# The attention sink as a column of the score rows, and one softmax step for both halves of a block

## The chip, the cores and the metric

The kernel runs on one core of a Trainium2 chip. A core has a matmul engine (TensorE, here PE), three elementwise engines (VectorE or DVE, ScalarE or ACT, GpSimd or POOL), a sequencer that issues most of the transfers (SyncE, SP), and on-chip memories SBUF and PSUM; matmuls write PSUM. Each engine works through its own list of instructions in order and waits on semaphores for the others. The metric is the device time of one execution in microseconds, the median of the runs shown.

## The reference

One layer of a hybrid decoder, for 1024 prompt tokens and 64 sample tokens, width 1024. One input projection feeds a sliding-window attention group and a state-space (SSD) group; their outputs go through one output projection, then a gated FFN. The attention is what the change touches:

```python
def sink_attention(q, k, v, valid, sinks):
    s = jnp.einsum('bnqkgd,bnskd->bnkgqs', q, k) * (HEAD_DIM ** -0.5)
    s = jnp.where(valid[None, :, None, None], s, -jnp.inf)
    sink = sinks.reshape(1, 1, ATT_KV_HEADS, ATT_GROUP, 1, 1)
    m = jnp.maximum(jnp.max(s, axis=-1, keepdims=True), sink)
    p = jnp.exp(s - m)
    den = jnp.sum(p, axis=-1, keepdims=True) + jnp.exp(sink - m)
    return jnp.einsum('bnkgqs,bnskd->bnqkgd', p / den, v)
```

The sink is one learned score per head. It takes part in the maximum and in the denominator, and has no value vector. A prompt query sees its own block of 128 keys and the block before, so a row of scores is 256 wide (128 in the first block); a sample query sees 192.

## The kernel before

Full precision comes from split operands: each matrix is a high part and a low part, and `gemm` (L140 to L142) makes three matmul passes. The prompt is cut into chunks of 384, 384 and 320 columns (the last holds the sample tokens).

The stage of the change begins about 466 us into the span and ends about 775 us in. There `weave` runs two programs on PE: the mixer (`attention`, later `att_sample`) and the filler (the z projection of the SSD gate, and after it the first output projection). The mixer yields a number, the time for which the filler may hold PE before the mixer goes on. This sets PE's list of instructions by hand. The lists of DVE, ACT, POOL and SP are ordered by a scheduler, from the program order and priorities; `tc.high_priority()` marks the steps that PE waits for soonest.

Attention has 16 blocks (n, p): n = 0 to 7 is a block of 128 queries, p one of two groups of 8 heads. Tiles are named after p: `a_0...` and `a_1...`. Each block does:

- `blk_a` loads q, k, v (SP), transposes v on PE (L737, `a_pvt`), and splits k into `KW` (ACT L742, DVE L743) and q into `A` (ACT L749, POOL L750).
- `blk_b` makes the scores (PE L768, tile `a_ps`, two PSUM buffers of two heads each), in two halves e = 0, 1 of four heads. DVE L774 adds the mask to a head's scores, writes them into the SBUF tile `a_pS` (one per half, four buffers) and takes the row maximum into `a_pmx`; each is two instructions, the reduce and a read of its accumulator. Then comes `softmax` (L709 to L723) for this half: `nm` = -max(mx/8, sink) (L711, 128x4), `es` = nm + sink (L713) and its exponential (ACT L714), four exponentials with the row sum into `den` (ACT L718), den + es (L719), reciprocal (L720), and four scalings of the rows in place (DVE L723).
- `blk_c` of the block *before* follows the scores on PE: for each half of the keys eight transposes (L792, `a_pt`: four heads of half 0, then four of half 1), copied out of PSUM as `a_pPT` (L113: half 0 by DVE, half 1 by ACT), then the product with v (L800, `a_po`) and its copy to `of` (ACT L805).

So the scalings of one block have to be there when PE, after the next block's scores, comes to their transposes. In between, the group norm of the SSD output (`gate`, L926 to L963) runs in pieces on DVE, ACT and POOL: `gz`, `gy` are its tiles, `g0...` its small norm tiles of the first chunk (L174 to L184, 128x6, and the diagonals `g0d` of L203, 128x128), `g1...` of the second. The filler's results leave PSUM by DVE (`stg`, L486), its weights `wi_0`, `wi_1` (later `wos`, `woa`) are split by ACT (L123) and by POOL or DVE (L124). All of these stand in the same lists as the softmax.

Of the kernel before, what the change touches and what calls it, by code (L numbers as in the profile page):

```python
# [34 lines left out]
def hybrid_layer(ctx, tc, A):  # L35
# [26 lines left out]
    # split operands of a chunk in half tiles of four feature tiles each, in numbered slots  # L62
# [37 lines left out]
    class Extra:  # L100
        # weight slots cut out of a larger tile
# [31 lines left out]
    def gemm(out, ws, xs, step=3, only=None):  # L133
        # three passes of split operands; yields the time on the tensor engine
# [18 lines left out]
    def weave(mixer, filler):  # L153
        # the filler yields its time on the tensor engine, or None while its operands are not there;
        # the mixer yields how long the filler may hold the tensor engine before it goes on
        credit = 0.0
        for gap in mixer:
            credit += gap
            while credit > 0:
                try:  # L160
                    cost = next(filler)
                except StopIteration:
                    break
                if cost is None:
                    break
                credit -= cost
# [4 lines left out]
    def rsqrt_cols(st, nb, inv, name):  # L171
        # 1/sqrt(st * inv + eps), one token per partition: bit-level first guess, Newton to float32
# [14 lines left out]
    def rms(groups, n, inv, name, gap, keep=None):  # L187
        # groups of tiles; the sum over a group's tiles and partitions is the sum of squares of each token
# [40 lines left out]
    # scratch in DRAM  # L229
# [106 lines left out]
    with pool("conv") as cvp:  # L336
# [38 lines left out]
        with pool("norm") as tp:  # L375
# [15 lines left out]
            # the tensor engine's clock comes up while the first operands are on their way  # L391
# [11 lines left out]
            def dt_mm(c, k):  # L403
                # four feature tiles at a time, in four column groups of the array
# [19 lines left out]
            # the first chunk by feature tile, as they come in; its evacuation waits for the row scale  # L424
# [82 lines left out]
    with pool("ssd") as sd, pool("rope") as rp:  # L507
# [5 lines left out]
        def ssd_a(c, gi):  # L513
            # token-major x scaled by dt and by the tail decay; masked C.B; decay weights
# [194 lines left out]
    def softmax(ap, mx, name, nh, nsk, sk, tile_w):  # L709
        nm = ap.tile([P, nh], F32, tag="nm", bufs=2, name=name + "nm")  # L710
        v.scalar_tensor_tensor(nm, mx, -0.125, nsk, ALU.mult, ALU.min)  # L711
        es = ap.tile([P, nh], F32, tag="es", bufs=2, name=name + "es")
        v.tensor_add(es, nm, sk)  # L713
        s.activation(es, es, AF.Exp)  # L714
        den = ap.tile([P, nh], F32, tag="den", bufs=2, name=name + "den")
        for h in range(nh):
            w = tile_w(h)
            s.activation(w, w, AF.Exp, bias=nm[:, h:h + 1], scale=0.125, accum_out=den[:, h:h + 1])  # L718
        v.tensor_add(den, den, es)  # L719
        v.reciprocal(den, den)  # L720
        for h in range(nh):
            w = tile_w(h)
# [31 lines left out]
    def blk_b(ap, n, p, KW, Aqs):  # L754
# [3 lines left out]
        Sms = [ap.tile([P, 4, 2 * P], F32, tag="Sm", bufs=4, name=nm + "S%d" % e) for e in range(2)]  # L758
# [3 lines left out]
        for e in range(2):  # L762
            for g2 in range(2):
# [6 lines left out]
                for a in range(2):  # L770
                    gi = 2 * g2 + a
                    h = 4 * e + gi
                    with tc.high_priority():
                        v.tensor_tensor_reduce(Sms[e][:, gi, :W], sq_[:, a, :W], cst[:, mcol:mcol + W],  # L774
                                               1.0, -3.0e38, ALU.add, ALU.max, mx[:, h:h + 1])
                yield 0.6
            o = 4 * e
            softmax(ap, mx[:, o:o + 4], nm, 4, nsink[:, 8 * p + o:8 * p + o + 4],
                    vec[:, V_SINK + 8 * p + o:V_SINK + 8 * p + o + 4], lambda h: Sms[e][:, h, :W])
        return Sms  # L780

    def blk_c(ap, n, p, vts, Sms):
# [4 lines left out]
        for kt in range(nk):  # L787
            PTs = []
            for e in range(2):
                tp_ = ps("t", nm + "t")  # L790
                for gi in range(4):
                    t.transpose(tp_[:, gi * P:gi * P + P], Sms[e][:, gi, kt * P:kt * P + P], ident)  # L792
# [15 lines left out]
    nsink = sp.tile([P, 17], F32, name="nsink")  # L808
    v.tensor_scalar_mul(nsink, vec[:, V_SINK:V_SINK + 17], -1.0)
# [26 lines left out]
    # sampled tokens: one batch row at a time, all heads on the rows  # L836
    def att_sample(ap):
        Qb = [ap.tile([P, NB, P], F32, name="Qb%d" % p) for p in range(2)]
        cv = ap.tile([P, NB, 2 * P], F32, name="cv")
        Ss = ap.tile([P, NB, 192], F32, name="Ss")  # L840
# [32 lines left out]
        for b2 in range(4):  # L873
# [7 lines left out]
            for i in range(2):  # L881
                b = 2 * b2 + i
                with tc.high_priority():
                    v.tensor_tensor_reduce(Ss[:, b, :], scs[:, i, :], mk[:, b, :], 1.0, -3.0e38, ALU.add, ALU.max, mx[:, b:b + 1])
            yield 1.7
            if b2 % 2:
                o = 4 * (b2 // 2)
                softmax(ap, mx[:, o:o + 4], "as%d" % b2, 4, nsink[:, 16:17].broadcast_to([P, 4]),
                        vec[:, V_SINKS:V_SINKS + 1].broadcast_to([P, 4]), lambda h: Ss[:, o + h, :])
# [3 lines left out]
        def tr(b2):  # L893
            tp_ = ps("t", "as%dt" % b2)
            for i in range(2):
                t.transpose(tp_[:, 2 * P * i:2 * P * i + P], Ss[:, 2 * b2 + i, :P], ident)
                t.transpose(tp_[:NS, 2 * P * i + P:2 * P * i + 2 * P], Ss[:, 2 * b2 + i, P:], ident)
# [30 lines left out]
    def gate(c, at=None):  # L928
        # y * silu(z), its norm, and the split of the result
# [131 lines left out]
    with pool("chain") as kp:  # L1061
        # the first FFN tiles go chunk by chunk
# [23 lines left out]
    with pool("ffn") as fp:  # L1086
        # the cache rows that only move up, in the time when little else is loaded
# [5 lines left out]
        for gi, G in enumerate(FFG):  # L1093
# [51 lines left out]
            else:  # L1145
                # the last feature tiles go chunk by chunk, with the last norm and the residual behind them
# [163 lines left out]
```

## Time and profile before

| | |
|---|---|
| runs | 1766.32, 1768.01, 1768.69 us |
| median | 1768.01 us |
| span of the profiled execution | 1755.4 us |
| median less the span | 12.6 us |
| PE busy | 1650.0 us, 94% |
| DVE / ACT / POOL busy | 931.4 / 629.0 / 659.3 us (53 / 36 / 38%) |

The profiled execution has no time of its own beside the three runs; its span, from the first instruction to the last, is 12.6 us under the median, and this difference is carried along unchanged. An engine's busy time is what its instructions took; PE's share of 94% is a mean over stages. The trace names, for every instruction that had to wait, what came last of the things that it waited for; "idle before" is that waiting time.

### The profile page before, as it was taken

To read this page: it belongs to the slowest core of one execution; us is meant where nothing else is said; L and a number is where in the kernel's file an instruction comes from. 1 tells how busy PE (TensorE), PEld (TensorE's weight loads), DVE (VectorE), ACT (ScalarE), POOL (GpSimd) and SP (SyncE) were. 2 spreads that over 40 slices of the span, in tenths; PEclk is the share of its full clock that TensorE was granted. 3 is DMA by queue.
4 is the path that set the end of the run, shared out by engine and by line. 5 is a ranking of instruction groups with operands and counts; after the bars stand their busy time and mean duration, and the time that the engine had idled before them with its cause. 6 is when DMAs were issued, how large, how long until landed. Compare 5 with 4: busy or idle time off the path is not lost. (4 is left out here: it accounts for less than half of the span.)

```text
span 1755.4 us, 26644 instructions
## 1 busy us (share of the span) xinstructions
PE 1650.0 (94%) x9959; PEld 1553.4 (88%) x9959; DVE 931.4 (53%) x1977; ACT 629.0 (36%) x1416; POOL 659.3 (38%) x537
## 2 busy tenths in 40 slices
PE   9899998888888998999988999999999999999995
PEld 6899987766776787898987999999999999999995
DVE  7796778886588898455877401221312212121347
ACT  5242344441376676554543332112121121211221
POOL 5262366666743333323655322222222221221432
PEclk9899999998999999999999999999999999999997
DMA  5022564444652351543554111111111111110233
GB/s 184 30 85 101 166 177 136 134 125 157 208 153 84 93 156 59 167 148 94 180 179 141 47 49 32 49 52 32 55 41 47 44 38 49 41 55 22 82 102 102
DMA packets 144945, 171.12 MB, mean 97 GB/s; under 512 B 16624, under 2 KB 105200, under 8 KB 144784
## 3 DMA queue, kind: packets, MB, share of 16 engines
q1 hardware_dynamic: 144816, 169.43, 31.6%
q8 instruction: 78, 1.28, 0.3%
q14 instruction: 51, 0.42, 0.1%
HBM read 135.33 MB, written 36.28 MB: 98 GB/s over the span
## 5 line engine op out<-in xcount | busy, mean ns | idle before, releaser
L1027 DVE TENSOR_TENSOR sg<-sg,ou 128x384 f32<-128x384 f32 (+1 forms) x66 | 35.0, 531 | 393.4 <-PE ou L142 392.7
L1138 DVE TENSOR_TENSOR YP<-YP,od 128x384 f32<-128x384 f32 (+1 forms) x168 | 89.0, 531 | 126.9 <-PE od L142 126.7
L124 POOL TENSOR_TENSOR wg_1l<-wg_1r,wg_1h 128x512 fp32r<-128x512 f32 x20 | 25.9, 1295 | 211.5 <-ACT wg_1h L123 211.5
L1028 ACT CAST ffh<-sg 128x384 fp32r<-128x384 f32 (+1 forms) x66 | 32.6, 495 | 188.9 <-DVE sg L1027 188.5
L124 POOL TENSOR_TENSOR wi_1l<-wi_1r,wi_1h 128x512 fp32r<-128x512 f32 x40 | 56.7, 1418 | 63.7 <-ACT wi_1h L123 60.2
L1023 ACT ACTIVATE sg<-og 128x384 f32<-128x384 f32 (+1 forms) x66 | 31.0, 471 | 131.9 <-PE og L142 125.2
L124 POOL TENSOR_TENSOR wi_0l<-wi_0r,wi_0h 128x512 fp32r<-128x512 f32 x40 | 58.3, 1458 | 30.6 <-ACT wi_0h L123 26.2
L1029 DVE TENSOR_TENSOR ffl<-sg,ffh 128x384 fp32r<-128x384 f32 (+1 forms) x66 | 42.8, 649 | 33.9 <-ACT ffh L1028 33.8
L140 PE MATMUL ip<-x1h,wi_0h 128*128 128x384 f32 x128 | 48.0, 375 | 11.8 <-ACT ra L681 5.2
L124 POOL TENSOR_TENSOR wos_1l<-wos_1r,wos_1h 128x512 fp32r<-128x512 f32 x24 | 33.1, 1377 | 65.3 <-ACT wos_1h L123 58.3
L124 POOL TENSOR_TENSOR woa_1l<-woa_1r,woa_1h 128x512 fp32r<-128x512 f32 x24 | 35.0, 1456 | 49.6 <-ACT woa_1h L123 38.4
L363 DVE SCALAR_TENSOR_TENSOR cacc<-cbuf,vec,cacc 128x1112 f32<-128x1112 f32 x36 | 52.3, 1455 | 0.7
L140 PE MATMUL ip<-x0h,wi_0h 128*128 128x384 f32 x128 | 47.4, 371 | 3.5 <-DVE cbuf L350 3.5
L124 POOL TENSOR_TENSOR wd_1l<-wd_1r,wd_1h 128x384 fp32r<-128x384 f32 (+1 forms) x7 | 6.8, 974 | 105.2 <-ACT wd_1h L123 105.2
L140 PE MATMUL ip<-x0h,wi_1h 128*128 128x384 f32 x128 | 45.6, 356 | 0.0
L142 PE MATMUL ip<-x0h,wi_0l 128*128 128x384 f32 x128 | 44.0, 344 | 1.5 <-POOL wi_0l L124 1.5
L140 PE MATMUL ip<-x1h,wi_1h 128*128 128x384 f32 x128 | 45.1, 353 | 0.0
L124 POOL TENSOR_TENSOR wg_0l<-wg_0r,wg_0h 128x512 fp32r<-128x512 f32 x21 | 27.4, 1304 | 45.6 <-ACT wg_0h L123 45.6
L142 PE MATMUL ip<-x1h,wi_0l 128*128 128x384 f32 x128 | 44.3, 346 | 0.0
L141 PE MATMUL ip<-x0l,wi_0h 128*128 128x384 f32 x128 | 43.8, 342 | 0.4 <-DVE x0l L261 0.4
L141 PE MATMUL ip<-x1l,wi_0h 128*128 128x384 f32 x128 | 44.2, 345 | 0.0
L684 POOL TENSOR_TENSOR rb<-rb,sinT 128x384 f32<-128x384 f32 (+1 forms) x30 | 36.0, 1198 | 21.2 <-DVE rb L683 17.5
(837 smaller groups left out, 6215.0 us busy)
## 6 DMA issues: line engine op xcount, KB each, us to landing
wi_0r<-in_w_in SPq DMA_DIRECT2D x40, 256.0 KB
wi_1r<-in_w_in SPq DMA_DIRECT2D x40, 256.0 KB
wos_0r<-in_w_os SPq DMA_DIRECT2D x24, 256.0 KB
wos_1r<-in_w_os SPq DMA_DIRECT2D x24, 256.0 KB
woa_0r<-in_w_oa SPq DMA_DIRECT2D x24, 256.0 KB
woa_1r<-in_w_oa SPq DMA_DIRECT2D x24, 256.0 KB
wg_0r<-in_w_g SPq DMA_DIRECT2D x22, 256.0 KB
wg_1r<-in_w_g SPq DMA_DIRECT2D x22, 256.0 KB
```

The source lines that it names most:

```text
L124: (eng or g).tensor_sub(lo, raw, fr(hi))
L140: t.matmul(out, lhsT=wh, rhs=xh, start=k == 0, stop=False)
L141: t.matmul(out, lhsT=wh, rhs=xl, start=False, stop=False)
L142: t.matmul(out, lhsT=wl, rhs=xh, start=False, stop=k == n - 1)
L363: v.scalar_tensor_tensor(acc[:, :L], buf[:, k:k + L], vec[:, cw + k:cw + k + 1], acc[:, :L], ALU.mult, ALU.add)
L684: g.tensor_mul(b, b, sinT[:, c0:c0 + n])
L1023: s.activation(sg, og[:, :n], AF.Silu)
L1027: v.tensor_mul(sg, sg, ou[:, :n])
L1028: s.copy(hi[:, c0:c0 + n], sg)
L1029: v.tensor_sub(lo[:, c0:c0 + n], sg, fr(hi[:, c0:c0 + n]))
L1138: v.tensor_add(YP[m][:, c0:c0 + n], YP[m][:, c0:c0 + n], o[:, :n])
```

## The change

- A tile `sink8` holds eight times the sink of each head (scores are scaled by 1/8 in the exponential). The tile `nsink` is gone.
- `a_pS` grows from 4x256 to 4x257 columns for each half. Column 0 of each row is the sink, copied there by two POOL instructions of 128x4 per block (L757 of the new file); scores start at column 1. For the samples, `Ss` grows from 192 to 193 columns, and one DVE copy fills the column.
- The reduce (L773) starts its maximum from the sink, read per partition from `sink8`, in place of a constant.
- `softmax` is called once per block, after both halves: one `nm` (L712, 128x8), eight exponentials of 257 columns (L715), one reciprocal (L716, 128x8), eight scalings (L719) of the 256 columns behind the sink. `es`, its exponential and the addition to `den` are gone, since the row sum contains the sink.
- The transposes (L789) read from column 1 on.

```diff
-    def softmax(ap, mx, name, nh, nsk, sk, tile_w):
+    def softmax(ap, mx, name, nh, row):
         nm = ap.tile([P, nh], F32, tag="nm", bufs=2, name=name + "nm")
-        v.scalar_tensor_tensor(nm, mx, -0.125, nsk, ALU.mult, ALU.min)
-        es = ap.tile([P, nh], F32, tag="es", bufs=2, name=name + "es")
-        v.tensor_add(es, nm, sk)
-        s.activation(es, es, AF.Exp)
+        v.tensor_scalar_mul(nm, mx, -0.125)
         den = ap.tile([P, nh], F32, tag="den", bufs=2, name=name + "den")
         for h in range(nh):
-            w = tile_w(h)
-            s.activation(w, w, AF.Exp, bias=nm[:, h:h + 1], scale=0.125, accum_out=den[:, h:h + 1])
-        v.tensor_add(den, den, es)
+            s.activation(row(h), row(h), AF.Exp, bias=nm[:, h:h + 1], scale=0.125, accum_out=den[:, h:h + 1])
         v.reciprocal(den, den)
         for h in range(nh):
-            w = tile_w(h)
+            w = row(h)[:, 1:]
             v.tensor_scalar_mul(w, w, den[:, h:h + 1])
...
-        Sms = [ap.tile([P, 4, 2 * P], F32, tag="Sm", bufs=4, name=nm + "S%d" % e) for e in range(2)]
+        Sms = [ap.tile([P, 4, 2 * P + 1], F32, tag="Sm", bufs=4, name=nm + "S%d" % e) for e in range(2)]
+        for e in range(2):
+            o = 8 * p + 4 * e
+            g.tensor_copy(Sms[e][:, :, 0:1], sink8[:, o:o + 4].unsqueeze(2))
...
-                        v.tensor_tensor_reduce(Sms[e][:, gi, :W], sq_[:, a, :W], cst[:, mcol:mcol + W],
-                                               1.0, -3.0e38, ALU.add, ALU.max, mx[:, h:h + 1])
+                        v.tensor_tensor_reduce(Sms[e][:, gi, 1:1 + W], sq_[:, a, :W], cst[:, mcol:mcol + W],
+                                               1.0, sink8[:, 8 * p + h:8 * p + h + 1], ALU.add, ALU.max, mx[:, h:h + 1])
                 yield 0.6
-            o = 4 * e
-            softmax(ap, mx[:, o:o + 4], nm, 4, nsink[:, 8 * p + o:8 * p + o + 4],
-                    vec[:, V_SINK + 8 * p + o:V_SINK + 8 * p + o + 4], lambda h: Sms[e][:, h, :W])
+        softmax(ap, mx, nm, 8, lambda h: Sms[h // 4][:, h % 4, :1 + W])
         return Sms
...
-                    t.transpose(tp_[:, gi * P:gi * P + P], Sms[e][:, gi, kt * P:kt * P + P], ident)
+                    t.transpose(tp_[:, gi * P:gi * P + P], Sms[e][:, gi, 1 + kt * P:1 + kt * P + P], ident)
...
-        Ss = ap.tile([P, NB, 192], F32, name="Ss")
+        Ss = ap.tile([P, NB, 193], F32, name="Ss")
+        v.tensor_copy(Ss[:, :, 0:1], sink8[:, 16:17].unsqueeze(1).broadcast_to([P, NB, 1]))
...
-                    v.tensor_tensor_reduce(Ss[:, b, :], scs[:, i, :], mk[:, b, :], 1.0, -3.0e38, ALU.add, ALU.max, mx[:, b:b + 1])
+                    v.tensor_tensor_reduce(Ss[:, b, 1:], scs[:, i, :], mk[:, b, :], 1.0, sink8[:, 16:17], ALU.add, ALU.max,
+                                           mx[:, b:b + 1])
...
-                softmax(ap, mx[:, o:o + 4], "as%d" % b2, 4, nsink[:, 16:17].broadcast_to([P, 4]),
-                        vec[:, V_SINKS:V_SINKS + 1].broadcast_to([P, 4]), lambda h: Ss[:, o + h, :])
+                softmax(ap, mx[:, o:o + 4], "as%d" % b2, 4, lambda h: Ss[:, o + h, :])
```

PE's list keeps its 8672 rows in the same order. The lists of the other engines are ordered anew by the scheduler. Three places follow. In these lists a name such as `a_0S_4805` is one half's tile of a block of p = 0, the next number the other half's.

DVE at block (1,0), before: the end of its softmax. `a_0S_4805` is half 0, `a_0S_4806` half 1; `a_1PT` belongs to the block before it.

```order
L720 RECIPROCAL a_0den<-a_0den 128x4
L723 TENSOR_SCALAR a_0S_4805<-a_0S_4805,a_0den 128x256
L113 COPY a_1PT<-a_1t 128x512
L723 TENSOR_SCALAR a_0S_4805<-a_0S_4805,a_0den 128x256 x3
L486 TENSOR_TENSOR stg<-ip,rs0Rk 128x384
L719 TENSOR_TENSOR a_0den<-a_0den,a_0es 128x4
L720 RECIPROCAL a_0den<-a_0den 128x4
L723 TENSOR_SCALAR a_0S_4806<-a_0S_4806,a_0den 128x256 x4
L743 TENSOR_TENSOR KW_4402<-a_0k,KW_4402 128x2x128
L774 ISA a_1S_4970,a_1mx<-a_1s,cst 128x256
```

DVE at the same block (1,0) now; half 0 is `a_0S_4785`, half 1 `a_0S_4786`, and `a_1S_4941` is half 1 of the next block, (1,1).

```order
L773 ISA a_1S_4941,a_1mx<-a_1s,cst,sink_4393 128x256
L773 ISA a_1mx 128x1
L486 TENSOR_TENSOR stg<-ip,rs0Rk 128x384
L719 TENSOR_SCALAR a_0S_4785<-a_0S_4785,a_0den 128x256 x2
L719 TENSOR_SCALAR a_0S_4786<-a_0S_4786,a_0den 128x256 x2
L113 COPY a_0PT<-a_0t 128x512
L719 TENSOR_SCALAR a_0S_4786<-a_0S_4786,a_0den 128x256 x2
L712 TENSOR_SCALAR a_1nm<-a_1mx 128x8
```

The last six scalings of the block moved from ahead of the next block's reduces to behind them, and the copy of the block's own first transposes now stands between the two pairs of half 1.

ACT around the first piece of the gate, before. `gz_0` is the gate's tile of 128x1536, `ACT_TABLE_LOAD` loads another set of functions, the two copies of `a_0PT` are those of block (1,0), `a_1S_4971` is half 1 of block (1,1).

```order
L749 CAST a_1A<-a_1q 64x512
L113 COPY a_0PT<-a_0t 128x512
L718 ACTIVATE a_1S_4971,a_1den<-a_1S_4971,a_1nm 128x256
L714 ACTIVATE a_1es<-a_1es 128x4
L718 ACTIVATE a_1S_4971,a_1den<-a_1S_4971,a_1nm 128x256 x3
L939 ACT_TABLE_LOAD
L939 ACTIVATE gz_0_5123<-gz_0_5123 128x1536
L113 COPY a_0PT<-a_0t 128x512
L805 COPY of_4390<-a_0o 128x4x128
```

ACT at the same place now (`a_1S_4940` and `a_1S_4941` are the two halves of block (1,1)).

```order
L745 CAST a_1A<-a_1q 64x512
L123 CAST wi_0h<-wi_0r 128x512
L938 ACT_TABLE_LOAD
L938 ACTIVATE gz_0_5083<-gz_0_5083 128x1536
L113 COPY a_0PT<-a_0t 128x512
L715 ACT_TABLE_LOAD
L715 ACTIVATE a_1S_4940,a_1den<-a_1S_4940,a_1nm 128x257 x3
L113 COPY a_0PT<-a_0t 128x512
L715 ACTIVATE a_1S_4940,a_1den<-a_1S_4940,a_1nm 128x257
L715 ACTIVATE a_1S_4941,a_1den<-a_1S_4941,a_1nm 128x257 x3
```

The gate's load of functions and its long activation moved from behind the first `a_0PT` copy to ahead of it, and the exponentials' functions are loaded once more behind it.

DVE at block (2,0), before, where the norm of the gate's first chunk runs. All scalings of block (2,0) stand ahead of these rows.

```order
L774 ISA a_1S_5377,a_1mx<-a_1s,cst 128x256
L774 ISA a_1mx 128x1
L113 COPY a_0PT<-a_0t 128x512
L183 SCALAR_TENSOR_TENSOR g0t<-g0t,g0y 128x6
L711 SCALAR_TENSOR_TENSOR a_1nm<-a_1mx,nsink 128x4 x2
L184 SCALAR_TENSOR_TENSOR g0y<-g0t,g0y 128x6
L713 TENSOR_TENSOR a_1es<-a_1nm,vec 128x4 x2
L203 TENSOR_SCALAR g0d<-cst,g0y 128x128 x4
L486 TENSOR_TENSOR stg<-ip,rs1Rk 128x384
L203 TENSOR_SCALAR g0d<-cst,g0y 128x128 x2
```

DVE at the same place now; `a_0S_5122` is half 1 of block (2,0).

```order
L113 COPY a_0PT<-a_0t 128x512
L182 TENSOR_TENSOR g0t<-g0m,g0y 128x6
L719 TENSOR_SCALAR a_0S_5122<-a_0S_5122,a_0den 128x256
L183 SCALAR_TENSOR_TENSOR g0t<-g0t,g0y 128x6
L719 TENSOR_SCALAR a_0S_5122<-a_0S_5122,a_0den 128x256
L184 SCALAR_TENSOR_TENSOR g0y<-g0t,g0y 128x6
L719 TENSOR_SCALAR a_0S_5122<-a_0S_5122,a_0den 128x256
L203 TENSOR_SCALAR g0d<-cst,g0y 128x128 x4
L486 TENSOR_TENSOR stg<-ip,rs1Rk 128x384
L203 TENSOR_SCALAR g0d<-cst,g0y 128x128 x2
L719 TENSOR_SCALAR a_0S_5122<-a_0S_5122,a_0den 128x256
```

The four scalings of half 1 moved behind the copy of half 0's transposes, the last of them behind the six diagonals and `stg`.

## Rows read from the trace of the kernel before

**Rows 1.** Stretches: start:end, length, busy us (instructions) by engine, granted clock, DMA.

```profile
466.20:775.00 308.80, 286.41 (x1716) 244.50 (x1715) 237.76 (x731) 205.46 (x551) 120.33 (x88) 0.97 0.43 131
775.00:1700.00 925.00, 901.09 (x5432) 895.96 (x5433) 309.31 (x563) 236.35 (x472) 268.55 (x222) 0.99 0.22 68
```

**Rows 2.** PE's waits, 460 to 780 us: us in total, times, longest.

```profile
PE ip L140 <- DVE stg L486: 3.6, 1, 3.6
PE a_0o L800 <- DVE a_0PT L113: 3.4, 5, 1.9
PE a_1o L800 <- DVE a_1PT L113: 3.1, 4, 1.3
PE a_1s L768 <- DVE a_1mx L774: 2.6, 3, 1.6
...
PE a_0o L800 <- ACT a_0PT L113: 1.9, 1, 1.9
PE a_1s L768 <- POOL a_1A L750: 1.7, 1, 1.7
...
PE a_0s L768 <- DVE a_0mx L774: 1.3, 1, 1.3
...
PE a_0t L792 <- DVE a_0S L723: 0.8, 1, 0.8
```

**Rows 3.** Groups on DVE, 460 to 775 us: count, busy us, mean ns, idle before.

```profile
L719 DVE TENSOR_TENSOR a_0den<-a_0den,a_0es 128x4 f32<-128x4 f32 x16 | 5.4, 339 | 5.8 <-ACT a_0S L718 5.8
...
L713 DVE TENSOR_TENSOR a_1es<-a_1nm,vec 128x4 f32<-128x4 f32 x16 | 5.2, 344 | 0.1
```

**Rows 4.** DVE's timeline in block (3,1): start us, us, instruction; POOL idle.

```profile
584.56 0.16 DVE L719 TENSOR_TENSOR a_1den<-a_1den,a_1es 128x4 f32<-128x4 f32 x1 [1.55 <-ACT a_1S L718]
584.75 0.18 DVE L720 RECIPROCAL a_1den<-a_1den 128x4 f32<-128x4 f32 x1
584.97 1.14 DVE L723 TENSOR_SCALAR a_1S<-a_1S,a_1den 128x256 f32<-128x256 f32 x4
```

**Rows 5.** DVE's timeline in block (0,1).

```profile
486.82 2.98 DVE L723 TENSOR_SCALAR a_1S<-a_1S,a_1den 128x128 f32<-128x128 f32 x4
```

**Rows 6.** POOL's timeline at the same time.

```profile
486.86 1.26 POOL L750 TENSOR_TENSOR a_1A<-a_1q,a_1A 64x512 fp32r<-64x512 f32 x1 [4.27 <-issue]
```

**Rows 7.** DVE's timeline: block (1,0), and a copy at block (2,0).

```profile
495.65 0.08 DVE L774 DVE_READ_ACCUMULATOR2_ANT a_0mx<- 128x1 f32 x1
...
501.28 2.18 DVE L723 TENSOR_SCALAR a_0S<-a_0S,a_0den 128x256 f32<-128x256 f32 x4
...
543.55 0.68 DVE L113 COPY a_0PT<-a_0t 128x512 f32<-128x512 f32 x1
```

**Rows 8.** PE's timeline: the first transposes of block (1,0).

```profile
506.86 1.04 PE L792 MATMUL a_0t<-cst,a_0S 128*128 128x128 f32 x8
```

**Rows 9.** ACT's timeline around the first piece of the gate.

```profile
509.51 0.57 ACT L113 COPY a_0PT<-a_0t 128x512 f32<-128x512 f32 x1
...
513.43 1.28 ACT L939 ACT_TABLE_LOAD   x1
514.72 1.48 ACT L939 ACTIVATE gz<-gz 128x1536 f32<-128x1536 f32 x1
```

**Rows 10.** All instructions of a line: ns shortest/median/longest, first and last start, forms.

```profile
L718 ACT ACTIVATE a_0S<-a_0S,a_0nm x64: 385/496/515, 471.9 to 694.0; 128x256 f32<-128x256 f32 x56, 128x128 f32<-128x128 f32 x8
...
L723 DVE TENSOR_SCALAR a_0S<-a_0S,a_0den x64: 275/348/1417, 474.1 to 696.6; 128x256 f32<-128x256 f32 x56, 128x128 f32<-128x128 f32 x8
...
L774 DVE CUSTOM_DVE_ANT_0 a_0S<-a_0s,cst x64: 278/416/425, 466.4 to 687.1; 128x256 f32<-128x256 f32 x56, 128x128 f32<-128x128 f32 x8
...
L346 POOL COPY cbuf<-cvs x12: 205/207/1259, 25.4 to 170.7; 128x24 f32<-128x24 f32 x12
```

**Rows 11.** A stretch as in Rows 1, after a wait of PE of 1.9 us.

```profile
486.50:489.60 3.10, 3.04 (x6) 1.02 (x7) 3.03 (x7) 1.56 (x4) 2.59 (x2) 0.52 0.12 31
```

More of the change, by code (lines that the diff above doesn't have):

```diff
@@ L806, in blk_c @@
         yield 1.0
-    nsink = sp.tile([P, 17], F32, name="nsink")
-    v.tensor_scalar_mul(nsink, vec[:, V_SINK:V_SINK + 17], -1.0)
+    sink8 = sp.tile([P, 17], F32, name="sink8")
+    v.tensor_scalar_mul(sink8, vec[:, V_SINK:V_SINK + 17], 8.0)
     for p in range(2):
@@ L895, in tr @@
             for i in range(2):
-                t.transpose(tp_[:, 2 * P * i:2 * P * i + P], Ss[:, 2 * b2 + i, :P], ident)
-                t.transpose(tp_[:NS, 2 * P * i + P:2 * P * i + 2 * P], Ss[:, 2 * b2 + i, P:], ident)
+                t.transpose(tp_[:, 2 * P * i:2 * P * i + P], Ss[:, 2 * b2 + i, 1:1 + P], ident)
+                t.transpose(tp_[:NS, 2 * P * i + P:2 * P * i + 2 * P], Ss[:, 2 * b2 + i, 1 + P:], ident)
             PT = ap.tile([P, 2, 2 * P], F32, tag="PTs", bufs=2, name="as%dPT" % b2)
```

## The prediction

> **What bounds the kernel now.** The first view is the table of stretches. In the attention stage PE is busy 286 of 309 us; DVE, the next, 238, ACT 205, POOL 120. In the 925 us behind it PE is busy 901 [rows 1]. So PE is the bound throughout, and what PE gains or loses in the stage is carried to the end of the span unchanged: nothing later has room to give it back or take it up. The change leaves PE's own list alone, so it can act only through PE's waits. The second view lists these waits: on DVE they come to 3.6 + 3.4 + 3.1 + 2.6 + 1.3 + 0.8 = 14.8 us, on ACT's copy 1.9, on POOL 1.7 [rows 2]. This is a ceiling: with a DVE that never kept PE waiting the kernel would win some 15 us, under 1%. The third view are the groups of DVE's instructions, the fourth the time lines of DVE, ACT and PE at the places where the lists changed.
>
> **Instructions removed on DVE.** Each of 16 blocks loses one `nm`, two `es`, two `den` additions and one reciprocal: 96 instructions. On a free engine they follow each other at (584.97 - 584.56)/2 = 0.2 us [rows 4], which makes 19 us. Ends: at the shortest duration shown, 0.16, 15 us; at the means of the groups, 0.34 for the 80 that are no reciprocals (one group of two is shown of each kind) and 0.18 for 16, 30 us [rows 3, 4]. I take 19, since the difference between 0.16 and 0.34 is not work of these instructions. A scaling shows where it comes from: four of 128 columns took 2.98 us while a POOL instruction of 1.26 us and the next one ran, four of 256 columns took 1.14 with POOL idle [rows 4 to 6]. DVE stands still while POOL works, and whichever DVE instruction comes next will stand still instead. [...]
>
> **Instructions added.** 32 POOL copies of 128x4; the nearest row, 128x24, has 0.21 us [rows 10], so at most 6.6 us of an engine that idles 188 us of the stage [rows 1]; below nothing there is no reason. They stand in POOL's list ahead of the block's reduces and need only that the block two before is transposed. Behind those transposes the mixer yields 1.5, 1.0 and 0.4 us before the scores, so 2.9 us hide two copies and one POOL instruction of 1.3 ahead of them; I take nothing, and without that cover it is up to 1.7 us for a block's first reduce. The reduce now reads its start per partition. The scaling reads such an operand too, and its 256 columns are shorter than the reduce's (0.35 against 0.42) [rows 10]; so I take nothing, and as the other end one more step like the accumulator's read, 0.08 [rows 7], by 128 = 10 us of DVE. ACT's exponentials grow by one column, 0.9 ns (496 less 385 over 128 columns) [rows 10], nothing; ACT also loses the 32 short ones and gains two loads of functions of 1.28 us [rows 9], one pair at the gate.
>
> **Rows that start on odd words.** With rows of 257 columns the scalings of heads 0 and 2 of each half start on an odd word. Today's scaling costs (348 - 275)/128 = 0.57 ns per column, the reduce (416 - 278)/128 = 1.08 [rows 10]. If the odd ones fell to the reduce's rate, each wide one would cost 0.13 more, 7 us on DVE over 56; if all fell, 15. No row before has such a start; every shown form runs at one of these rates, and I take no loss. [...]
>
> **The longer way from maximum to scaling.** This is the cost. Before, half 0 went ahead while half 1 had its scores. Behind the last maximum stood `nm` and `es` 0.4, four exponentials 2.0, `den` and reciprocal 0.4, four scalings 1.1: 3.9 us. Now it is `nm` 0.2, eight exponentials 4.0, reciprocal 0.2, eight scalings 2.3: 6.7 us [rows 4, 10]. In block (1,0) the last maximum is there at 495.7, the last scaling was at 503.5, and PE transposes at 506.9 [rows 7, 8]. A room of 11.2 us would hold 6.7; but DVE's list now puts the last six scalings behind the next block's reduces, which follow scores that PE makes just ahead of the transposes, and the copy of half 0's transposes between the scalings of half 1. That copy waits for PE, and PE's next transposes wait for the scalings behind it: copy 0.6 (0.68 with its start [rows 7]), two scalings 0.6, a hop: some 1.2 us. This split stands in six blocks: (0,1), (1,0), (1,1), (2,0), (3,1), (6,0).
>
> **The sum over places.**
> Block (0,0): the copy behind PE's wait of 1.9 [rows 2] no longer stands behind a string of small instructions: -2.0.
> (0,1): split +1.2, the wait of 1.3 on its copy absorbed: 0.
> (1,0): split, and half 0's last two scalings behind the reduces: +2.0.
> Gate: the first `a_0PT` copy of ACT, at 509.51, now stands behind a load of 1.28 and an activation of 1.48 [rows 9], of which some 0.5 starts earlier: +2.2; the old wait of 1.9 on the second copy [rows 2] goes: +0.3.
> (1,1): split +1.2, one of the waits of 1.3 absorbed: 0.
> (2,0): behind the copy stand, before the last scaling, three others 0.8, three small ones 0.6, six diagonals at a scaling's pitch 1.6, `stg` 0.6, with the copy 0.6 and the scaling itself 0.3: 4.5, of which 0.5 runs before PE asks. A wait of 4.0 takes the place of 0.8 + 3.6 [rows 2]: -0.4.
> (3,0) to (5,1): split +1.2, less the 2.0 left of the waits on PT copies (3.4 + 3.1 less 1.9 and twice 1.3): -0.8.
> (6,0): behind six diagonals 1.6 and a weight split 0.7 now come eight scalings 2.3 and the copy 0.6, 1.1 of which has time: +4.1; the waits on POOL's `a_1A` 1.7 and on `a_1mx` 1.6 [rows 2], just ahead, go since both come earlier: +0.8.
> (7,0): the wait of 1.3 on `a_0mx` [rows 2]: -1.3.
> Together -1.4; against the median 1768.0 that is 1766.6. The difference of 12.6 us between median and span stays. [...]
>
> **Rivals.**
> *The relief wins* (0.27). DVE has 19 us less to do, so it reaches the copies and scalings early enough that the splits cost nothing. For: DVE is busy 77% of the stage and most of PE's waits are on it [rows 1, 2]. Against: the splits are an order, not a load; an emptier DVE only waits longer at the copy. Of 14.8 all but the 4.4 of (2,0) goes, and 2 at the gate, while 3 of new holds stay: -9.4, 1758.6.
> *The late halves* (0.21), slower. The place is the transposes of half 1 in the six split blocks: the price is 1.2 each with nothing absorbed, 7.5, and beyond the split 1.0 at (1,0), 2.7 at (2,0), 2.8 at (6,0), 2.2 at the gate; old waits that go take off 1.9, 4.4, 3.3: +6.6, 1774.6. It decides from where the last scaling of half 1 ends after PE has done half 0's transposes, in a block whose products had not been waiting.
> *The odd rows* (0.06), slower: all scalings at 1.08 ns per column. The 15 us take most of the 19 back and every block's scalings end 8 x 0.13 = 1 us later, felt in about seven blocks: -1.4 + 7 = +5.6, less what is absorbed, 1773.
> *Nothing moves* (0.06): the old waits stem from DVE standing still for POOL and only change their address; no relief and no split: 1768.
>
> **How the numbers follow.** My forecast has 0.40, with 1762 to 1771 as its own range. Two runs of this kernel can be told apart from about 0.2%, 3.5 us. Faster by more (below 1764.5): the relief 0.27 and 0.07 of the forecast's low end, 0.34. Within: 0.31 of the forecast and 0.06 of the nothing, 0.37. Slower (above 1771.5): 0.21 + 0.06 + 0.02 of the forecast's high end, 0.29. The range reaches to the relief's and the late halves' times, 1758.5 to 1774.5, which leaves out the farther part of each, some 0.2 together.
>
> **What the next profile would show.** Right: no wait of 1.9 in block (0,0); waits of PE on `a_pS` scalings (L719) in the split blocks of 1 to 1.5 us each, and one of some 4 at (2,0); a wait on ACT's `a_0PT` near 510 us; two loads of functions more; DVE busy some 19 us less in the stage, scalings at 0.35 us. Wrong: PE's waits on L719 hardly to be seen (then the relief), or over 10 us of them (the late halves), scalings of heads 0 and 2 near 0.48 (the odd rows), PE waiting for reduces that wait for POOL's copies (the cover of 2.9 us fails).

## The result, and the profile after

The changed kernel is slower: 1778.64 us in the median (1776.83 to 1781.19) against 1768.35 for four runs of the kernel before, ratio 1.0075 with a 95% interval of 1.0056 to 1.0094. That is 10 us more by the medians and 13 by the ratio. It lies above the forecast range of 1758.5 to 1774.5, and the kernel became slower where the forecast of 1766.6 had it slightly faster.

The stage is compared first, from the first v transpose of the attention to the first product of the samples, so that both rows cover the same PE instructions. The stretch table of the kernel before (start:end, length, busy us by engine with instruction counts, granted clock):

```profile
465.64:775.76 310.12, 286.97 (x1719) 245.06 (x1720) 238.68 (x733) 206.22 (x553) 121.64 (x89) 0.97 0.43 131
```

And of the changed one:

```profile
469.47:795.12 325.65, 293.89 (x1719) 250.49 (x1720) 225.00 (x633) 206.84 (x520) 125.26 (x117) 0.94 0.41 124
```

The order of columns after the length is PE, weight loads, DVE, ACT, POOL, then the clock. The stage is 15.5 us longer. The same 1719 matmul records took 293.9 in place of 287.0 us, so 6.9 us went to a lower granted clock, and PE stood idle 31.8 in place of 23.1 us, 8.6 more. DVE has 13.7 us less to do, as intended. A second trace of the kernel before has 310.3 us for this stage, so the difference is no accident of one execution. The whole spans do vary: 1755.4 and 1761.2 us before, 1776.3 after, where the changed kernel's own time of that execution was 1778.55, 2.2 us above its span. The 12.6 us that I carried along as lying outside the span were mostly this: the trace of before came from an execution shorter than the runs beside it. Therefore ratios of runs are used below, and traces for where the time lies.

PE's waits in the changed kernel, 460 to 800 us (us in total, times, longest), beside [rows 2]:

```profile
PE a_0t L789 <- DVE a_0S L719: 12.3, 10, 2.7
PE a_1t L789 <- DVE a_1S L719: 9.5, 7, 2.2
...
PE a_1t L789 <- DVE a_1PT L113: 2.2, 1, 2.2
...
PE a_0t L789 <- DVE g0t L183: 1.4, 1, 1.4
...
PE a_0t L789 <- ACT a_1A L745: 0.9, 1, 0.9
PE a_1o L797 <- DVE a_1PT L113: 0.7, 1, 0.7
PE a_0o L797 <- DVE a_0PT L113: 0.7, 3, 0.3
PE a_0o L797 <- ACT a_0PT L113: 0.5, 1, 0.5
PE a_0t L789 <- ACT wi_0h L123: 0.4, 1, 0.4
```

The wait of 3.6 on `stg` and the 1.7 on POOL's `A` are gone; the 8.4 on the copies of the transposes, DVE's and ACT's, in front of the products are down to 1.9. In their place PE waits 21.8 us, 17 times, for the scalings of the softmax. The three waits of transposes that the trace puts down to `g0t`, `A` and `wi_0h`, 2.7 us, are of the same kind: in each the transpose started 0.15 us behind the end of the scaling that it reads.

Block (1,0) shows how. DVE's timeline (start us, us, instruction):

```profile
506.77 2.40 DVE L719 TENSOR_SCALAR a_0S<-a_0S,a_0den 128x256 f32<-128x256 f32 x2
509.09 0.47 DVE L773 CUSTOM_DVE_ANT_0 a_1S<-a_1s,cst,sink 128x256 f32<-128x256 f32 x1
...
510.71 0.54 DVE L486 TENSOR_TENSOR stg<-ip,rs0Rk 128x384 f32<-128x384 f32 x1
511.18 3.01 DVE L719 TENSOR_SCALAR a_0S<-a_0S,a_0den 128x256 f32<-128x256 f32 x4
514.11 0.68 DVE L113 COPY a_0PT<-a_0t 128x512 f32<-128x512 f32 x1
514.71 0.60 DVE L719 TENSOR_SCALAR a_0S<-a_0S,a_0den 128x256 f32<-128x256 f32 x2
```

POOL's at the same time:

```profile
506.34 1.30 POOL L124 TENSOR_TENSOR wi_1l<-wi_1r,wi_1h 128x512 fp32r<-128x512 f32 x1 [3.06 <-ACT wi_1h L123]
507.72 1.29 POOL L746 TENSOR_TENSOR a_0A<-a_0q,a_0A 64x512 fp32r<-64x512 f32 x1
509.09 1.26 POOL L746 TENSOR_TENSOR a_1A<-a_1q,a_1A 64x512 fp32r<-64x512 f32 x1
510.43 1.27 POOL L124 TENSOR_TENSOR wi_0l<-wi_0r,wi_0h 128x512 fp32r<-128x512 f32 x1
512.19 1.84 POOL L939 TENSOR_TENSOR gy<-gy,gz 128x768 f32<-128x768 f32 x1 [0.49 <-DVE a_0S L719]
```

And PE's:

```profile
509.31 0.30 PE L789 MATMUL a_0t<-cst,a_0S 128*128 128x128 f32 x1 [0.36 <-ACT wi_0h L123]
512.00 0.97 PE L789 MATMUL a_0t<-cst,a_0S 128*128 128x128 f32 x3 [2.38 <-DVE a_0S L719]
514.24 0.47 PE L789 MATMUL a_0t<-cst,a_0S 128*128 128x128 f32 x1 [1.27 <-DVE a_0S L719]
515.10 0.74 PE L789 MATMUL a_0t<-cst,a_0S 128*128 128x128 f32 x2 [0.38 <-DVE a_0S L719]
515.49 0.67 PE L140 MATMUL ip<-x1h,wi_0h 128*128 128x384 f32 x1
```

In the trace of before these eight transposes took 1.04 us with no wait [rows 8]. Now the eight scalings come in three pieces, the first two of them while POOL instructions run: 6.0 us where 2.3 would do with POOL idle [rows 4]. Between the first two pieces stand four reduces of block (1,1), and these are not held: the one at 509.09 took its 0.47 us beside POOL's 1.26. PE waits 4.4 us at the transposes, and then the granted clock is low (0.51):

```profile
515.50:518.20 2.70, 2.70 (x11) 2.70 (x10) 1.08 (x2) 2.24 (x3) 0.00 (x0) 0.51 0.41 75
```

### The profile page after: what moved, and what is told of

Its sections match the earlier page's. It is cut to its first block, busy times and chain, and to the rows that moved or that the text cites. A ratio compares the mean times of both kernels' runs of the same rounds, so it can differ in the third digit from the quotient of the medians.

```text
span 1776.3 us, 26617 instructions
## 1 busy us (share of the span) xinstructions
PE 1662.4 (94%) x9959; PEld 1562.4 (88%) x9959; DVE 916.8 (52%) x1878; ACT 629.3 (35%) x1384; POOL 663.2 (37%) x569
```

## The experiments

Ratios are to the kernel before, run on the same chip beside each kernel. Theory L: the merging of the two halves makes the scalings late, and PE pays for it. Rival C: the column itself costs it.

**The kernel before once more.**

> The kernel before, unchanged, run beside itself, for a second trace of it. The trace at hand has a span of 1755.4 us, 12.6 us under the median time, while the changed kernel's span of 1776.3 lies 2.2 us under the time of its own execution. If the trace at hand was a lucky execution, this one shows a span some 2 us under its time, about 1764 to 1767, and shows where the luck lay (granted clock of some stretches, or a wait). If spans of this kernel always lie 12 us under the time, it shows about 1755 again. Ratio 1.000 in either case.

1764.02 against 1767.25, ratio 0.9984 (0.9968 to 1.0000), a span of 1761.2. So two sets of runs of one kernel may differ by 0.16%, and the first trace was some 6 us on the short side. The stage has the same length in both traces.

**Softmax by halves, the column kept.**

```diff
-        softmax(ap, mx, nm, 8, lambda h: Sms[h // 4][:, h % 4, :1 + W])
+            softmax(ap, mx[:, 4 * e:4 * e + 4], nm, 4, lambda h: Sms[e][:, h, :1 + W])
```

> The changed kernel, with the softmax called for each half of four heads as before; the sink column, the reduce that starts from the sink and the POOL copies stay, and so does the saving of es, its exponential and the addition. Theory L (late halves: the merging of the two halves makes the scalings late, and the lists of DVE and ACT that follow from it hold PE): the loss goes, 1764 to 1770 us, PE's waits on scalings L719 fall from 21.8 us to under 4. Rival C (the column costs it: each of 128 reduces takes 0.06 us longer with its start read per partition, POOL's copies, odd rows): the loss stays, 1775 to 1779, and the waits on L719 with it.

1757.69, ratio 0.9948 (0.9928 to 0.9968). That is below the range of L, which only had the loss go: the kernel is faster than the one before. PE's waits on scalings are one:

```profile
PE a_0t L789 <- DVE a_0S L719: 0.8, 1, 0.8
```

At block (1,0) DVE's and PE's timelines are:

```profile
500.51 2.64 DVE L719 TENSOR_SCALAR a_0S<-a_0S,a_0den 128x256 f32<-128x256 f32 x4
...
506.79 1.03 PE L789 MATMUL a_0t<-cst,a_0S 128*128 128x128 f32 x8
```

The last four scalings are drawn out here too (2.64 us in place of 1.14 [rows 4]), but end at 503.2, 3.6 us ahead of PE. The column and its reduce are in this kernel, so C falls.

**Merged, without the column.**

```diff
-            o = 4 * e
-            softmax(ap, mx[:, o:o + 4], nm, 4, nsink[:, 8 * p + o:8 * p + o + 4],
-                    vec[:, V_SINK + 8 * p + o:V_SINK + 8 * p + o + 4], lambda h: Sms[e][:, h, :W])
+        softmax(ap, mx, nm, 8, nsink[:, 8 * p:8 * p + 8],
+                vec[:, V_SINK + 8 * p:V_SINK + 8 * p + 8], lambda h: Sms[h // 4][:, h % 4, :W])
```

> The kernel before, with no sink column and no POOL copies, but with one softmax for both halves (nm, es, its exponential, den and reciprocal once as 128x8, behind both halves). Theory L: as slow as the changed kernel or slower, 1775 to 1782 us, PE waits on the scalings L723 of 15 us or more. Rival C: near the kernel before, 1764 to 1770, with waits on L723 of about 1 us as before.

1787.81, ratio 1.0113 (1.0090 to 1.0135), slower still than the range that L gave. Its waits:

```profile
PE a_0t L791 <- DVE a_0S L723: 13.7, 11, 3.0
PE a_1t L791 <- DVE a_1S L723: 8.2, 9, 2.3
```

The merging alone does the harm. The changed kernel, with the column, is at 1.0075; the two intervals overlap a little.

**The split around DVE's copy taken out.**

```diff
-                    on(s if e else v, (PT, tp_))
+                    on(v if e else s, (PT, tp_))
```

> The changed kernel, with the copies of the transposes out of PSUM exchanged: half 0 by ACT, half 1 by DVE. DVE's copy then needs the transposes of half 1, so all eight scalings stand ahead of it and the split between two pairs is gone in all six blocks. If the split is the greater part of the loss, half of it or more goes: 1770 to 1774 us. If the lateness itself is (eight exponentials and the reduces ahead of the scalings), the time stays at 1776 to 1781, PE's waits move onto fewer and longer ones on L719.

1775.04, ratio 1.0049 (1.0030 to 1.0068), between the two ranges: by the ratios about a third of the loss goes, with overlapping intervals, and in the traces the stage is 323.5 us, so 2.1 of its 15.5 us are gone. The waits on scalings are 19.0 us (12.8 and 6.2). The split that I priced as the cost is the smaller part of it.

**Early exponentials, late scalings.** `nm` and the exponentials by halves, the reciprocal (128x8) and the eight scalings behind both.

```diff
-        softmax(ap, mx, nm, 8, lambda h: Sms[h // 4][:, h % 4, :1 + W])
+            if e == 0:
+                den = ap.tile([P, 8], F32, tag="den", bufs=2, name=nm + "den")
+            ng = ap.tile([P, 4], F32, tag="nm", bufs=4, name=nm + "nm")
+            v.tensor_scalar_mul(ng, mx[:, 4 * e:4 * e + 4], -0.125)
+            for h in range(4):
...
+        v.reciprocal(den, den)
+        for h in range(8):
...
```

> The changed kernel with the maximum, nm and the four exponentials of each half at once, as before, and only the reciprocal (128x8) and the eight scalings behind both halves. The exponentials of half 0 no longer wait for half 1's scores. If the late exponentials are the loss, most of it goes: 1757 to 1764 us against 1767 before, PE's waits on the scalings under 8 us. If it is that all eight scalings stand in one place behind the reduces and around DVE's copy, most of it stays: 1770 to 1778, waits on the scalings 14 us or more. The list of DVE keeps the split in six blocks, so I lean to the second, 1772.

1777.64, ratio 1.0070 (1.0046 to 1.0094): all of the loss stays, more than the 1772 that I leaned to. Waits on scalings 19.5 us:

```profile
PE a_0t L799 <- DVE a_0S L786: 11.5, 9, 3.5
PE a_1t L799 <- DVE a_1S L786: 8.0, 8, 2.1
```

**Late exponentials, scalings by halves**, the complement.

```diff
-        softmax(ap, mx, nm, 8, lambda h: Sms[h // 4][:, h % 4, :1 + W])
+        ng = ap.tile([P, 8], F32, tag="nm", bufs=2, name=nm + "nm")
+        v.tensor_scalar_mul(ng, mx, -0.125)
+        for e in range(2):
+            den = ap.tile([P, 4], F32, tag="den", bufs=4, name=nm + "den")
...
+            v.reciprocal(den, den)
...
```

> The complement of the run with early exponentials: the changed kernel with one nm for both halves, so the exponentials stay late, but reciprocal and scalings for each half of four heads. If the merged reciprocal, which makes half 0's scalings wait for half 1's exponentials, is what the merging costs, more than half of the loss goes: 1758 to 1768 us, PE's waits on scalings under 10. If anything that makes the scalings late costs the same, it stays above 1772. In DVE's list half 0's scalings now stand ahead of the next block's second reduces in most blocks, but the split remains in some, so I expect 1766.

1766.15, ratio 1.0008 (0.9989 to 1.0027), as expected. Waits on scalings 6.7 us:

```profile
PE a_0t L799 <- DVE a_0S L786: 5.3, 4, 2.5
...
PE a_1t L799 <- DVE a_1S L786: 1.4, 1, 1.4
```

Read against the kernel by halves (0.9948): late exponentials alone cost 0.6%, a merged reciprocal alone 1.2%, both together 1.3%. The two are no sum. With a merged reciprocal half 0's scalings wait for half 1's exponentials, and that costs nearly all of it; with late exponentials they wait for half 1's maxima only, and that costs half.

**More room for late scalings.** PE's order edited: filler between the scores and the transposes of the block before.

```diff
             if i > 0:
+                yield 2.4
                 yield from blk_c(ap, *blocks[i - 1], vts, Sm.pop(blocks[i - 1]))
...
-        yield 1.0
+        yield 0.0
```

> The changed kernel with the order of PE alone edited: 2.4 us of filler between the scores of a block and the transposes of the block before, and the 1.0 us behind the product taken out. Theory L says that PE waits because the scalings come late by 1 to 3 us per block and that work in between covers it: 1762 to 1772 us, PE's waits on L719 from 21.8 to under 10. If the lateness is not the cause, the time stays at 1775 to 1782.

1797.38, ratio 1.0183 (1.0157 to 1.0209). The waits on scalings did fall, from 21.8 to 8.6 us:

```profile
PE a_0t L789 <- DVE a_0S L719: 8.0, 7, 2.0
...
PE a_1t L789 <- DVE a_1S L719: 0.6, 1, 0.6
```

Up to the v transpose of block (2,1) this kernel had lost 2.1 us against the kernel before since the start of the stage, the changed one 7.0. Its whole stage is longer, but holds more work, 1845 matmul records in place of 1719:

```profile
467.02:800.44 333.42, 309.16 (x1845) 266.16 (x1846) 233.27 (x644) 215.09 (x537) 136.52 (x123) 0.97 0.42 129
```

The filler's products start 0.174 us apart, so the 126 more are some 22 us, an estimate from this trace. Without them the stage would be some 311 us, close to the kernel before and not to the changed one. But behind the stage, from where that filler was taken, PE stood 22 us in one wait:

```profile
PE pf1st L195 <- DVE acc L992: 22.1, 1, 22.1
```

So the time missed its range, and only the waits and the stage speak for the theory. The same with 1.0 us, the gaps' sum unchanged:

> The changed kernel with 1.0 us of filler moved from behind a block's product to ahead of its transposes; the sum of the gaps is unchanged, so the filler lasts as long as before, unlike in the run with 2.4 us, where it ran out and PE waited 22 us later on. Theory L: each of some ten late blocks gets 1.0 us covered, 1768 to 1774 us, PE's waits on L719 near 12 to 15 us. If lateness is not what PE pays for, 1776 to 1782.

1790.70, ratio 1.0151 (1.0120 to 1.0183), and the waits on scalings did not fall (25.1 us):

```profile
PE a_0t L789 <- DVE a_0S L719: 16.9, 11, 5.4
PE a_1t L789 <- DVE a_1S L719: 8.2, 10, 1.4
```

This expectation failed. The scheduler made the lists of DVE anew around the other order of PE, so the edit did not change the room alone; the stage was as long as in the changed kernel to about 1 us, and the rest was lost behind it, 6.2 us of it in a wait of PE for ACT's `sg` in the FFN that the changed kernel does not have. That filler in between cures the lateness is not shown.

**The start read per partition.** The kernel before, its reduce started from a column.

```diff
+    low = sp.tile([P, 1], F32, name="low")
+    g.memset(low, -3.0e38)
...
-                                               1.0, -3.0e38, ALU.add, ALU.max, mx[:, h:h + 1])
+                                               1.0, low[:, 0:1], ALU.add, ALU.max, mx[:, h:h + 1])
```

> The kernel before, with the reduce's start read per partition from a column of -3e38 in place of the constant; rows are 256 wide and start even. If the operand costs 0.06 us, the reduce takes 0.477 instead of 0.416 and DVE has 8 us more; PE waits on the reduces and on DVE's copies in some of the blocks, so 0 to 5 us more than before, 1767 to 1772. If the reduce stays at 0.416, the 257-column rows were the reason.

1770.76, ratio 1.0041 (1.0022 to 1.0059). The time is in its range, but it is 6.5 us above the kernel before beside it, where 0 to 5 had been expected. The reduce (shortest/median/longest ns):

```profile
L774 DVE CUSTOM_DVE_ANT_0 a_0S<-a_0s,cst,low x64: 323/479/485, 470.7 to 699.9; 128x256 f32<-128x256 f32 x56, 128x128 f32<-128x128 f32 x8
```

416 had become 479 [rows 10] with even rows of 256. The operand costs the 0.06 us, not the odd start.

**The same undone: column, halves, start from a constant.** In the kernel by halves, the reduce from -3.0e38 and `nm` as before the change:

```diff
-        v.tensor_scalar_mul(nm, mx, -0.125)
+        v.scalar_tensor_tensor(nm, mx, -0.125, nsk, ALU.mult, ALU.min)
...
-                                               1.0, sink8[:, 8 * p + h:8 * p + h + 1], ALU.add, ALU.max, mx[:, h:h + 1])
+                                               1.0, -3.0e38, ALU.add, ALU.max, mx[:, h:h + 1])
```

> The kernel with the sink column and the softmax for each half (the one that measured 1757.7), but the reduce starts from a constant again and the sink comes into nm by the two-operand instruction, as before the change. If the start read per partition is what made the reduce 0.06 us longer, the reduce falls from 0.477 to 0.416 us, DVE has 128 x 0.06 = 8 us less to do, and the time is 0 to 4 us under the 1757.7. If the longer reduce came from the odd start of the rows it writes, it stays at 0.477 and so does the time.

1756.11, ratio 0.9939 (0.9916 to 0.9961), the fastest of all, 0.6% under the kernel before. The reduce is back, with rows that start odd:

```profile
L773 DVE CUSTOM_DVE_ANT_0 a_0S<-a_0s,cst x64: 280/418/428, 468.3 to 681.2; 128x256 f32<-128x256 f32 x56, 128x128 f32<-128x128 f32 x8
```

The step from 0.9948 to 0.9939 is inside the intervals, so the 8 us of DVE bought no measurable time here. With the 1.0 us of filler moved it lost again:

> The sink column with the softmax for each half and the reduce from a constant (1756.1), with the same 1.0 us of filler moved ahead of the transposes. There PE hardly waits on scalings, so there is little to cover: 1753 to 1758; what moves are the waits on DVE's copies of the transposes (6.4 us) that follow less filler behind them.

1770.60, ratio 1.0022 (0.9998 to 1.0046): outside its range, and again what was lost lay behind the stage, 7.3 us of it in that wait for `sg`.

**Merged, column, start from a constant.** The same edit on the changed kernel.

> The changed kernel, still with one softmax for both halves, but with the reduce from a constant and the sink in nm by the two-operand instruction (128x8). It fills the last place of the table merged or by halves, column or not, start from a constant or per partition. The costs seem to add up so far: merging about +20 us with and without the column, the column -10. If the start per partition costs what it did on the kernel before (+4 to +7), this runs at 1771 to 1775 against 1778.6; if as little as by halves (1.6), at 1776 to 1779. PE's waits on the scalings stay near 20 us either way, since nothing is done about the merged reciprocal.

1775.68, ratio 1.0046 (1.0024 to 1.0068), between its two ranges, and by its ratio 0.3% under the changed kernel, with overlapping intervals. The waits on scalings are 19.2 us. The table of ratios is now full but for one place:

| | no column, constant | no column, per partition | column, constant | column, per partition |
|---|---|---|---|---|
| by halves | 1 | 1.0041 | 0.9939 | 0.9948 |
| merged | 1.0113 | | 1.0046 | 1.0075 |

Down a column the merging costs 1.1 to 1.3%, 19 to 22 us. From the first to the third the sink column, with what it makes superfluous, brings 0.6 to 0.7%, some 11 us. The start per partition costs 0.1 to 0.4%. The change is all three together. The stage's length in the traces tells the same: by halves 310.1, 317.9, 299.4 and 303.0 us in the table's order, merged 330.2, 324.8 and 325.7.

## Why the prediction was wrong

**The reading of the bound was right.** The difference arose in the attention stage, as PE's waits and PE's clock, and was carried to the end. PE's shift between the two traces is +3.8 us at the start of the stage, +19.4 at its end and +20.8 close to the end of the span; against the second trace of the kernel before it is +1.3, +16.7 and +15.1.

**The relief was there, and smaller.** I took 19 us off DVE; 128 reduces took 0.06 longer, 8 us of it back, and the stage shows 13.7 less. The reason given, that whichever DVE instruction comes next stands still for POOL, does not hold for the reduces: none of the 128 took over 0.49 us, though 69 of the 112 wide ones ran at least partly beside an instruction of POOL. Taking nothing for the operand was wrong, on the reason that another instruction with such an operand is quick; its stated end of 10 us was near. And the relief pays: by halves the column wins 0.6%, close to the -9.4 us of the rival that had it win.

**The sum over places failed,** which was to be -1.4 and came to +15.5 in the traces. It is worked out from where PE's v transposes start in each, as the change of the shift from one block's to a later one's:

| transposes of block | forecast | traces |
|---|---|---|
| start of the stage | 0 | -0.9 |
| (0,0) | -2.0 | -3.1 |
| (0,1) | 0 | +2.3 |
| (1,0) and gate | +2.3 | +3.1 |
| (1,1) | 0 | +5.5 |
| (2,0) | -0.4 | +0.7 |
| (2,1) to (5,1) | -0.8 | +9.2 |
| (6,0) | +0.8 | +2.4 |
| behind it | -1.3 | -3.8 |

With the second trace of the kernel before the entries move by up to 1.1 us. Of the 16.9 us between forecast and traces, 10.0 are PE's idle time (8.6 us more where 1.4 less had been forecast) and 6.9 the clock.

*The step that failed is where PE would be held.* The prediction saw that DVE's list puts the last six scalings behind the next block's reduces, but let "a room of 11.2 us" hold the 6.7 us of the longer way. So it charged a block for what stands behind DVE's copy of the first transposes, the split (1.2 us), and ahead of that copy only 0.8 at (1,0) and some 2.9 at (6,0). PE's waits for scalings at the first eight transposes of these blocks are:

| block | new holds forecast | waits ahead of the copy | waits behind it |
|---|---|---|---|
| (0,0) | 0 | 2.9 | no split |
| (0,1) | 1.2 | 1.9 | 0.5 |
| (1,0) | 2.0 | 4.0 | 0.4 |
| (1,1) | 1.2 | 2.1 | 2.2 |
| (2,0) | 4.0 | 1.1 | 3.0 |
| (3,1) | 1.2 | 2.2 | 0.6 |
| (6,0) | 4.1 | 2.7 | 0.6 |

Behind the copy, where 10.0 us were forecast, PE waited 7.3. Ahead of it, where 3.7 were, it waited 16.9. Block (3,1) shows the common case. DVE's timeline has three scalings, then four reduces of block (4,0), then the last scaling of half 0:

```profile
603.07 1.97 DVE L719 TENSOR_SCALAR a_1S<-a_1S,a_1den 128x256 f32<-128x256 f32 x3
...
606.57 1.88 DVE L719 TENSOR_SCALAR a_1S<-a_1S,a_1den 128x256 f32<-128x256 f32 x3
```

PE's:

```profile
608.07 0.77 PE L789 MATMUL a_1t<-cst,a_1S 128*128 128x128 f32 x3 [2.18 <-DVE a_1S L719]
609.41 0.59 PE L789 MATMUL a_1t<-cst,a_1S 128*128 128x128 f32 x2 [0.58 <-DVE a_1S L719]
```

In the trace of before half 0's four scalings of this block ended at 586.1 [rows 4], and PE came to them without a wait:

```profile
591.94 1.03 PE L792 MATMUL a_1t<-cst,a_1S 128*128 128x128 f32 x8
```

*The price of a late scaling was too low as well, "two scalings 0.6".* They were priced at the pitch of a free engine, although the rows with 2.98 and 1.14 us for four stood in the argument [rows 4 to 6]. I used them to hold down the relief and left them out of the cost. In block (1,1) they met POOL's `gy`, `wi_1l` and `A`. DVE's timeline:

```profile
528.62 3.18 DVE L719 TENSOR_SCALAR a_1S<-a_1S,a_1den 128x256 f32<-128x256 f32 x2
...
532.53 0.68 DVE L113 COPY a_1PT<-a_1t 128x512 f32<-128x512 f32 x1
533.13 1.61 DVE L719 TENSOR_SCALAR a_1S<-a_1S,a_1den 128x256 f32<-128x256 f32 x2
```

PE's:

```profile
530.68 0.30 PE L789 MATMUL a_1t<-cst,a_1S 128*128 128x128 f32 x1 [1.20 <-DVE a_1S L719]
531.86 0.47 PE L789 MATMUL a_1t<-cst,a_1S 128*128 128x128 f32 x1 [0.88 <-DVE a_1S L719]
534.53 0.74 PE L789 MATMUL a_1t<-cst,a_1S 128*128 128x128 f32 x2 [2.20 <-DVE a_1S L719]
```

A wait of 4.3 us stands where 1.2 less 1.3 was put down. All scalings together are as busy as before (51.6 against 51.3 us), so they were stretched as much then; only nobody waited for them. In both traces every scaling of 256 columns that took over 0.5 us ran beside POOL's instructions (9 of 112 before, up to 1.44 us; 12 of 112 now, up to 1.92), and those with POOL idle took 0.34 to 0.36 us. The reduces of 256 columns took 0.47 to 0.49 us in the changed kernel, beside POOL and with it idle. The stretched scalings belonged in the price of lateness.

*"Absorbed" failed too.* I let new holds swallow the old waits on the copies at (0,1) and (1,1). The old ones went, as said, and the holds were far larger.

The experiments fit this: without the split (the exchanged copies) 19.0 of the 21.8 us of waits on scalings stay, and the two complements show that half 0's scalings, once they wait for half 1's exponentials, cost nearly the whole loss.

*The clock was in no term of the sum,* although [rows 11] show 3.1 us at 0.52 behind a wait. The stage's matmuls took 6.9 us more at a mean granted clock of 0.94 instead of 0.97; 2.7 us behind the holds of (1,0) ran at 0.51. By the granted clock of the trace 37.5 us of the stage ran at 0.5, against 17.1 before, and six of its eight stretches began during or just behind the holds of the six split blocks. Idle time in sum does not tell: the run with late exponentials had 29.3 us of it in the stage, at 0.97.

**The rivals.** The late halves came true, with 0.21 and 1774.6 (six splits of 1.2 are 7.2, not 7.5, so 1774.3), and were priced too low for the same reasons: 21.8 us of waits on scalings against "over 10". About half of the waits stood at another place than this rival said, the transposes of half 0. The gate was no such place: PE did not wait there for ACT's copy, where 2.2 us had been put down, since that copy itself waited 3.8 us for PE's late transposes:

```profile
515.93 0.59 ACT L113 COPY a_0PT<-a_0t 128x512 f32<-128x512 f32 x1 [3.82 <-PE a_0t L789]
```

The odd rows fell. By heads of a half, the medians of the scalings of 256 columns are 351, 348, 348 and 347 ns, against 353, 348, 347 and 346 before; heads 0 and 2 start on an odd word now. With POOL idle, as in block (2,1), all eight of a block took 2.19 us:

```profile
565.75 2.19 DVE L719 TENSOR_SCALAR a_1S<-a_1S,a_1den 128x256 f32<-128x256 f32 x8
```

By these rows a start on an odd word costs a scaling nothing here: four that all start even took 1.14 us before [rows 4]. POOL's copies cost nothing, as said: PE never waited for one, and they took 0.19 us each in the median.

**What stays open.** How much of the lateness is the scheduler's placing of the scalings behind the next block's reduces, and how much the dependence itself, was not separated: each edit changed all lists, and moving 1.0 us of filler alone shifted the time by 0.8% in two kernels, as much as some of the differences in the table. How much of the loss comes of scalings drawn out beside POOL was read from the rows, and not tried by taking POOL's work away. Behind the stage the two kernels by halves with the column take 987 us, where the two traces of the kernel before take 980 and 983, so a part of what they win in the stage (7 and 11 us) is lost there; why was not looked into.

## What to carry to other kernels

Fusing small instructions over two halves of a block saves their time on an engine with time to spare and spends the early half's head start; ask first who waits for the second half's result, and in whose list it then stands. Price a step that becomes late by what stands ahead of it there and at what it takes beside the other work of its new place, not at what it takes alone, and count the clock: here 37.5 us of the stage ran at a granted 0.5, against 17.1 before. The two parts of this change were best taken apart: the sink as a column brings 0.6%, the merging costs twice that, and the version by halves with a constant start is the one to keep.

## What the runs showed of the hardware

With a per-partition start value the fused reduce took some 0.06 us longer at both widths: 479 ns in the median for 256 columns in the run with that operand alone, where 416 stood before [rows 10], and for 128 columns means of 347 and 345 ns in the changed kernel, where the one before has 283 and 278. An odd start of its output rows, or of the scalings' rows, cost nothing (418 ns from a constant against 416; 351 and 348 where the row starts odd, 348 and 347 where it starts even). A group of two scalings on DVE beside POOL's instructions took up to 3.18 us in place of 0.6, while a fused reduce kept its 0.47 us beside them. And two traces of one kernel differ by 6 us of span, so that a single trace is no base for a sum of a few us over the whole span, while the stage's length agreed to 0.2.
